# Rotary embedding on one core: a longer fp32 lead of x, and three positions' results stored early in fp32

## The chip, the cores and the metric

One core of one Trainium2 chip. The metric is the device time of one execution in microseconds (us), as a median over executions; for kernels compared here they ran on the same chip in alternating rounds. "Span" is the profiled execution's own length, some 1.7 us shorter than the device time.

## The reference

```python
# x: (8, 2048, 16, 64) float32; cos, sin: (2048, 32)
x1, x2 = x_pairs[..., 0], x_pairs[..., 1]        # even and odd elements
out1 = x1 * cos - x2 * sin
out2 = x1 * sin + x2 * cos
out  = stack([out1, out2], axis=-1)              # same shape as x, float32
```

67.1 MB come in and 67.1 MB go out; each element sees three arithmetic operations.

## The kernel before

A batch of x is a tile of 128 partitions, each with 16 positions of 1024 elements (64 KB of fp32 in memory). Loads and stores go through GpSimd's DMA queue, which casts: fp32 in memory, bf16 on chip. VectorE rotates with three operations for each half of a batch, into a result buffer. There are three buffers for x and three for results. Load b and store b are those of batch b; load 3 reuses the buffer of batch 0, so it is issued only when VectorE is done with batch 0. Exceptions are at the ends: the first positions of batch 0 (the "lead") and the tables come in fp32 over the SP and ACT queues into one of the x buffers, and the last four positions leave in fp32.

A "row" is what one partition gets or gives in one transfer. In the packet records one data packet is one row, and a transfer's 128 rows are 8 for each of the 16 DMA engines. The records call GpSimd's queue q0 ("the software queue"), SP's q1 and ACT's q10. An engine with rows of several queues takes them in turn; a "turn" of q0 is the time of one of its rows.

```python
    with tc.manual_schedule():
        pre = fp32_tile()                            # takes the first x buffer
        ...
        for k in range(HEAD):                        # HEAD = 2: two positions, 4 KB rows
            q = (nc.sync, nc.scalar)[k % 2]
            q.dma_start(out=pre[:, k : k + 1], in_=x_t[0, :, k : k + 1])
        nc.sync.dma_start(out=cos_sb, in_=cos_t)     # tables behind the lead, in `pre` too
        nc.scalar.dma_start(out=sin_sb, in_=sin_t)
        load(0, HEAD)                                # GpSimd queue: rest of batch 0
        load(1)
        nc.scalar.copy(out=xs[0][:, :HEAD], in_=pre[:, :HEAD])
        ...                                          # VectorE builds the bf16 tables
        load(2)                                      # reuses the buffer of `pre`
        for b in range(B):
            os[b] = opool.tile([P, K, HD], bf16, name="ot")
            for k0 in range(0, K, KP):               # KP = 8
                rotate(b, k0, k0 + KP)
            if b + NX < B:
                load(b + NX)                         # reuses the buffer of batch b
            store(b, K if b < B - 1 else K - TAIL)
        ...                                          # the tail: fp32 over SP
```

## Time and profile before

| | before |
|---|---|
| device time | 317.46 us, three runs 317.38 to 317.55 |
| VectorE busy | 212.8 us of a span of 315.7 |
| DMA engines | 16, with work from 1.75 to 314.42 us |
| memory traffic | 134.7 MB, 427 GB/s over the span |

One more view: the DMA issues of the kernel before (destination <- source, issuing queue, count, KB each on the on-chip side, us from issue to landing).

```profile
xt<-in_x_dram ACTq DMA_DIRECT2D x1, 512.0 KB, 5.0
xt<-in_x_dram SPq DMA_DIRECT2D x1, 512.0 KB, 4.9
xt<-in_sin_dram ACTq DMA_DIRECT2D x1, 256.0 KB, 22.7
xt<-in_cos_dram SPq DMA_DIRECT2D x1, 256.0 KB, 18.3
```

The lead lands in 5 us. The tables, half its size and issued 0.4 us later, need 18 and 23: they share the engines with the long rows of GpSimd's queue.

### The profile page before, as it was taken

Reading aid. Unit: us, or ns where it says so; the run is one execution under the profiler, and the core shown is the slowest. Engines: PE = TensorE matmul, PEld = TensorE weight load, DVE = VectorE, ACT = ScalarE, POOL = GpSimd, SP = SyncE. Lnnn points to the kernel's source line nnn. Section 1 sums busy time; section 2 is a strip of 40 time slices with the busy share of each in tenths; the row PEclk is TensorE's granted clock in tenths of the full one; section 3 lists DMA queues with packets and bytes.
Section 4 is the critical chain, followed back from the end, with each engine's and each line's share of the span. In section 5 each row is a group of like instructions: output and inputs, shape, how many; then the busy total and the mean of one; then the engine's idle time right before and its main releaser. Section 6 shows DMA issues by size and latency. Waiting matters only on the chain.

```text
span 315.7 us, 146 instructions
## 1 busy us (share of the span) xinstructions
DVE 212.8 (67%) x51; ACT 6.9 (2%) x4; POOL 8.8 (3%) x20
## 2 busy tenths in 40 slices
DVE  0009999999999999619992299913999049990000
ACT  2100000000000000000000000000000000000400
POOL 1000001000100100100001000000000000000000
DMA  9999999999999999999999999999999999999996
GB/s 269 212 246 203 199 212 253 199 199 237 361 465 332 199 257 407 399 332 262 203 399 440 357 199 199 482 448 266 199 316 415 399 399 523 407 399 457 423 434 280
DMA packets 3024, 101.71 MB, mean 322 GB/s; under 512 B 336, under 2 KB 336, under 8 KB 848
## 3 DMA queue, kind: packets, MB, share of 16 engines
q0 software_dynamic: 2304, 98.04, 97.0%
q1 hardware_dynamic: 432, 2.88, 2.4%
q10 hardware_dynamic: 288, 0.79, 0.6%
HBM read 67.63 MB, written 67.11 MB: 427 GB/s over the span
## 4 chain that ended last, share of the span: by engine, by line
another core or an unknown queue 61%; DMA 16%; DVE 9%; ACT 1%; issue 0%; POOL 0%; ACTq 0%
DMA out_dram<-ot 16%; DVE xt L76 3%; DVE ot L81 3%; DVE ot L75 3%; ACT xt L117 1%; DVE c_tab L100 0%; POOL xt L57 0%; ACTq L116 0%; ACT ot L116 0%; ACTq L117 0%
## 5 line engine op out<-in xcount | busy, mean ns | idle before, releaser
L75 DVE TENSOR_TENSOR ot<-xt,c_tab 128x8192 bf16<-128x8192 bf16 x16 | 70.7, 4420 | 45.8 <-DMA out_dram<-ot 45.7
L81 DVE TENSOR_TENSOR ot<-ot,xt 128x8192 bf16<-128x8192 bf16 x16 | 70.8, 4425 | 0.5
L76 DVE TENSOR_TENSOR xt<-xt,s_tab 128x8192 bf16<-128x8192 bf16 x16 | 70.8, 4425 | 0.5
L98 DVE CAST s_tab<-xt 128x512 bf16<-128x512 f32 x1 | 0.5, 454 | 23.8 <-DMA xt<-in_sin_dram 23.8
L57 POOL DMA_DIRECT2D xt<-in_x_dram x8 | 4.4, 547 | 161.4 <-DVE ot L81 137.4
L60 POOL DMA_DIRECT2D out_dram<-ot x8 | 4.3, 535 | 113.8 <-DVE ot L81 113.8
L116 ACT COPY ot<-ot 1x1 bf16<-1x1 bf16 x1 | 0.2, 193 | 286.6 <-DMA out_dram<-ot 286.6
L117 ACT CAST xt<-ot 128x4096 f32<-128x4096 bf16 x1 | 3.6, 3604 | 0.0
L96 ACT CAST xt<-xt 128x2048 bf16<-128x2048 f32 x1 | 1.9, 1897 | 0.0
L96 ACT ACT_TABLE_LOAD x1 | 1.3, 1283 | 5.7 <-DMA xt<-in_x_dram 5.7
L100 DVE CAST c_tab<-xt 128x1024 bf16<-128x1024 f32 x1 | 0.7, 683 | 0.0
L99 DVE TENSOR_SCALAR s_tab<-xt 128x512 bf16<-128x512 f32 x1 | 0.4, 442 | 0.0
L133 POOL MEMSET const-float32-0.0<- 128x1 f32 x1 | 0.1, 98 | 0.2 <-issue 0.2
L133 POOL MEMSET const-bfloat16-1.0<- 128x1 bf16 x1 | 0.1, 101 | 0.0
L133 POOL MEMSET const-float32-1.0<- 128x1 f32 x1 | 0.1, 98 | 0.0
L133 POOL MEMSET const-uint8-127<- 128x1 uint8 x1 | 0.1, 98 | 0.0
## 6 DMA issues: line engine op xcount, KB each, us to landing
xt<-in_x_dram POOLq DMA_DIRECT2D x7, 4096.0 KB, 42.8
out_dram<-ot POOLq DMA_DIRECT2D x1, 6144.0 KB, 28.0
xt<-in_x_dram POOLq DMA_DIRECT2D x1, 3584.0 KB, 22.8
out_dram<-xt SPq DMA_DIRECT2D x1, 2048.0 KB, 15.5
xt<-in_x_dram ACTq DMA_DIRECT2D x1, 512.0 KB, 5.0
xt<-in_x_dram SPq DMA_DIRECT2D x1, 512.0 KB, 4.9
xt<-in_sin_dram ACTq DMA_DIRECT2D x1, 256.0 KB, 22.7
xt<-in_cos_dram SPq DMA_DIRECT2D x1, 256.0 KB, 18.3
```

Source lines behind the costliest of these rows:

```text
L57: nc.gpsimd.dma_start(out=xs[b][:, k0:], in_=x_t[b, :, k0:])
L60: nc.gpsimd.dma_start(out=out_t[b, :, :k1], in_=os[b][:, :k1])
L75: nc.vector.tensor_tensor(out=rows(op), in0=rows(xp), in1=tab(c_tab), op=mult)
L76: nc.vector.tensor_tensor(out=rows(xp), in0=rows(xp), in1=tab(s_tab), op=mult)
L81: nc.vector.tensor_tensor(out=o3, in0=o3, in1=x_swap, op=add)
L96: nc.scalar.copy(out=xs[0][:, :HEAD], in_=pre[:, :HEAD])
L98: nc.vector.tensor_copy(out=s2[:, :, 0], in_=sin_sb)
L99: nc.vector.tensor_scalar_mul(s2[:, :, 1], sin_sb, -1.0)
L100: nc.vector.tensor_copy(out=c_tab.rearrange("p k (i j) -> p (k i) j", j=2), in_=cos_sb.to_broadcast([P, K * D2, 2]),)
L116: nc.scalar.copy(out=os[B - 2][:1, 0, :1], in_=os[B - 1][:1, K - 1, :1])
L117: nc.scalar.copy(out=tail[:, :TAIL], in_=os[B - 1][:, K - TAIL :])
L133: nc = _bacc.Bacc("TRN2", target_bir_lowering=False, num_devices=1)
```

## The change

What it seems meant to do (the diff doesn't say): use the quick SP and ACT queues for more of the first x, so that VectorE has something to do early, and let the first results leave early, before the casting store of batch 0. The early results are an fp32 copy that ScalarE makes in one of the result buffers. The lead's two transfers now bring two positions each, in rows of 8 KB.

```diff
-    HEAD = 2
+    HEAD = 4
+    LEAD = 3
...
-        for k in range(HEAD):
-            q = (nc.sync, nc.scalar)[k % 2]
-            q.dma_start(out=pre[:, k : k + 1], in_=x_t[0, :, k : k + 1])
+        lead = fp32_tile(opool, "ot")[:, :LEAD]
+        for q, k0 in ((nc.sync, 0), (nc.scalar, HEAD // 2)):
+            q.dma_start(out=pre[:, k0 : k0 + HEAD // 2], in_=x_t[0, :, k0 : k0 + HEAD // 2])
...
-            for k0 in range(0, K, KP):
-                rotate(b, k0, k0 + KP)
+            cuts = [0, KP, K]
+            if b == 0:
+                rotate(b, 0, HEAD)
+                nc.scalar.copy(out=lead, in_=os[b][:, :LEAD])
+                for k in range(LEAD):
+                    nc.sync.dma_start(out=out_t[b, :, k : k + 1], in_=lead[:, k : k + 1])
+                cuts = [HEAD, KP, K]
+            for k0, k1 in zip(cuts, cuts[1:]):
+                rotate(b, k0, k1)
             if b + NX < B:
                 load(b + NX)
-            store(b, K if b < B - 1 else K - TAIL)
+            store(b, LEAD if b == 0 else 0, K if b < B - 1 else K - TAIL)
```

More of the change, by code (lines that the diff above doesn't have):

```diff
@@ L49, with fp32_tile @@
     xs, os = {}, {}
-    def fp32_tile():
-        return xpool.tile([P, K // 2, HD], fp32, name="xt")
+    def fp32_tile(pool, name):
+        return pool.tile([P, K // 2, HD], fp32, name=name)
     def load(b, k0=0):
@@ L57, in load, with store @@
         nc.gpsimd.dma_start(out=xs[b][:, k0:], in_=x_t[b, :, k0:])
-    def store(b, k1=K):
-        nc.gpsimd.dma_start(out=out_t[b, :, :k1], in_=os[b][:, :k1])
+    def store(b, k0=0, k1=K):
+        nc.gpsimd.dma_start(out=out_t[b, :, k0:k1], in_=os[b][:, k0:k1])
     def rotate(b, k0, k1):
@@ L83 @@
     with tc.manual_schedule():
-        pre = fp32_tile()
+        pre = fp32_tile(xpool, "xt")
+        lead = fp32_tile(opool, "ot")[:, :LEAD]
         cos_sb = pre[:, HEAD, : K * D2]
         sin_sb = pre[:, HEAD + 1, : K * D2]
-        for k in range(HEAD):
-            q = (nc.sync, nc.scalar)[k % 2]
-            q.dma_start(out=pre[:, k : k + 1], in_=x_t[0, :, k : k + 1])
+        for q, k0 in ((nc.sync, 0), (nc.scalar, HEAD // 2)):
+            q.dma_start(out=pre[:, k0 : k0 + HEAD // 2], in_=x_t[0, :, k0 : k0 + HEAD // 2])
         nc.sync.dma_start(out=cos_sb, in_=cos_t)
@@ L106 @@
             os[b] = opool.tile([P, K, HD], bf16, name="ot")
-            for k0 in range(0, K, KP):
-                rotate(b, k0, k0 + KP)
+            cuts = [0, KP, K]
[7 more added lines that the diff above has]
+                rotate(b, k0, k1)
             if b + NX < B:
                 load(b + NX)
-            store(b, K if b < B - 1 else K - TAIL)
-        tail = fp32_tile()
+            store(b, LEAD if b == 0 else 0, K if b < B - 1 else K - TAIL)
+        tail = fp32_tile(xpool, "xt")
         nc.scalar.copy(out=os[B - 2][:1, 0, :1], in_=os[B - 1][:1, K - 1, :1])
```

## The prediction

> **What bounds the kernel now.** I read the page first: engine shares, the row of DMA busy tenths, the queues.
>
> ```profile
> DVE 212.8 (67%) x51; ACT 6.9 (2%) x4; POOL 8.8 (3%) x20
> ...
> DMA  9999999999999999999999999999999999999996
> ...
> q0 software_dynamic: 2304, 98.04, 97.0%
> q1 hardware_dynamic: 432, 2.88, 2.4%
> q10 hardware_dynamic: 288, 0.79, 0.6%
> HBM read 67.63 MB, written 67.11 MB: 427 GB/s over the span
> ```
>
> VectorE (DVE) is busy for 67%; the DMA engines are at nine tenths or more in 39 of 40 slices. The row of GB/s swings between about 200 and 523, but that is an artefact: the MB column counts a casting load at its bf16 size. On the HBM side everything moves at 427 GB/s for the whole span. The packet records say the same for one engine: a load row of 64 KB (written as 32 KB of bf16) takes 2.432 us, a store row of 64 KB 2.449, a load row of 56 KB 2.129, a store row of 48 KB 1.83 to 1.85, a 16 KB fp32 row 0.611, a 4 KB fp32 row 0.159, a 2 KB row 0.084. So time goes with the fp32 bytes, about 0.037 ns a byte and 8 ns a packet, whether cast or not and whether software or hardware made the descriptors. I counted the packets in flight: none before 1.75 us, 15.4 of 16 on average from 2 to 4 us, then 16 or more at every stretch up to 312 us (the records of neighbours overlap by some 20 ns, hence 16.16 on average). The last data packet ends at 314.42 us, the span at 315.7. The DMA engines idle some 1.9 us at the start, under 0.15 us from 2 us to 312 us, and the last rows run out unevenly after that.
>
> Second, the waits (who waited for whom: us in total, times, longest), and then three lines of the timeline (start, duration, in brackets the idle time before it): VectorE's start, the load issued at the end of the first batch, the first wait for a result buffer.
>
> ```profile
> POOL xt L57 <- DVE ot L81: 137.4, 5, 35.1
> ...
> DVE ot L75 <- DMA out_dram<-ot: 45.7, 4, 12.1
> DVE s_tab L98 <- DMA xt<-in_sin_dram: 23.8, 1, 23.8
> ```
>
> ```profile
> 23.85 0.45 DVE L98 CAST s_tab<-xt 128x512 bf16<-128x512 f32 x1 [23.85 <-DMA xt<-in_sin_dram]
> ...
> 52.20 0.53 POOL L57 DMA_DIRECT2D xt<-in_x_dram  x1 [25.93 <-DVE ot L81]
> ...
> 140.95 4.42 DVE L75 TENSOR_TENSOR ot<-xt,c_tab 128x8192 bf16<-128x8192 bf16 x1 [9.53 <-DMA out_dram<-ot]
> ```
>
> VectorE waits at two places. It starts at 23.85 because the sine table lands late, and from batch 4 on (140.95, 179.53, 218.23, 256.88) it waits for a result buffer still being stored. Neither costs DMA time: meanwhile the software queue has rows to move. A batch is 39.0 us of DMA (8 rows an engine of 2.432 and 8 of 2.449) against 26.5 us of VectorE (6 of 4.42), so the queue lengthens with every batch. The time is the DMA's total work plus its first 2 us and last 1.3.
>
> **What the Trainium skill says.** (1) "DMA: Bandwidth & Descriptors", section "Where 436 GB/s comes from": 16 ports give 435 GB/s. The trace agrees: 65,536 bytes in 2.432 us on 16 engines is 431, and 427 over the span leaves nothing to win. (2) Same page, "Issuing engines are not separate DMA queues": DMAs from the scalar, sync and gpsimd engines run on the same 16 engines and interleave; several issuers save only issue time. So a second queue for the lead adds no bandwidth. The trace agrees as far as one engine's records go: the 4 KB rows of q1 and q10 alternate, 159 ns each, one at a time. (3) Same page, "Queues, rings and completion order": each engine goes round its queues packet by packet. In the trace a packet record is a whole row, so a small row can wait for a long one: the 2 KB table rows, issued at 1.15 us, take until 16.96 (cosine) and 21.34 us (sine), as each turn of q0 lasts 2.13 us. (4) Same page, "SWDGE vs HWDGE vs iDMA": only DMAs from GpSimd cast. So results that leave over SP need an fp32 copy, here by ScalarE.
>
> **The change, part by part**, in us per DMA engine. 128 rows over 16 engines is 8 rows of each transfer.
> - Lead: 16 rows of 4 KB go (16 x 0.159 = 2.54), 16 rows of 8 KB come (between 0.159 and 0.611 by bytes: 0.310 each, 4.95).
> - First casting load: 56 KB rows (8 x 2.129 = 17.03) become 48 KB (2.129 less a quarter of the step 2.432 - 2.129 for each 2 KB; 1.826 each, 14.61).
> - First store: 64 KB rows (8 x 2.449 = 19.59) become 52 KB (1.84 + 0.25 x 0.61 = 1.99 each, 15.94).
> - Early fp32 stores: 3 x 8 rows of 4 KB, 24 x 0.159 = 3.82.
> - Sum: 39.32 - 39.16 = +0.16. Some extra semaphore packets of 10 to 40 ns make it about 0.2. The bytes in HBM are the same.
>
> So the direct effect is nothing, unless DMA idle time goes away or appears. To take away: between 4 and 6 us I count no idle, so the 1 MB lead already fills the engines until the software queue delivers (first q0 packet at 5.31). A lead twice as long bridges a hole that isn't there. The first 1.9 us are issue latency (SP and ACT issue at 0.74, first packet 1.75) and remain. The tail is unchanged.
>
> To appear: VectorE's schedule moves, and if the software queue runs dry, that costs span.
> - *Start.* The lead takes 4.95 us from 2.0, to about 7. If q0 still joins at 5.3, two or three x rows per queue each wait for a turn of 1.83, and then the tables need 8 turns: 5.3 + 8 x 1.83 + 3 x 2.43 + about 3 of small rows = 30. If q0 joins only behind the lead, at 7.3: 7.3 + 8 x 1.83 + about 1.5 = 23.5, as before. (On one engine six cosine rows ran in succession with sine rows already issued, so rows seem to be committed ahead; I lean to the second.) VectorE starts at 24 to 31.
> - *First batch.* Tables 1.4, then 6 half-size operations of about 2.24 (half of 4.42 plus an estimated 0.03) and 3 full: 26.7 rather than 26.5. It ends at 52 to 60; before, 51.9. ScalarE's early copy of 3072 elements costs 2.75 (between 1.90 for 2048 and 3.60 for 4096) beside VectorE.
> - *First danger.* The work given to the queues without the next load, with the early stores, is 4.95 + 1.4 + 14.61 + 2 x 19.4 + 3.8 + 2 = 65.6, so they are dry at about 65 us. The next load is issued at 52.5 to 60 and needs at most 4 us to its first packet (1.25 to 5.31, the only such time the trace shows). Slack: 1 to 9 us.
> - *Second danger.* The early stores' buffer is handed to batch 2. Their 24 rows and 3 semaphore packets take turns with q0's 64 KB rows, so they need about three q0 transfers (two loads of 20.7 with the small rows, the short store of 17): issued at 36 to 42, first row perhaps 8 us later (the tail, issued at 299.29, had its first row at 305.41), landed at 99 to 111. Batch 2 was ready for its buffer at 79: a new VectorE wait of 15 to 30 us. It then ends at 126 to 138 (before: 104.5), and load 5 is issued there. The queue, with load 4 and store 1, is dry at 140.2. Slack: 13 down to -2 us.
> - From batch 5 on VectorE waits for stores at the same times as before, and the delay is absorbed.
>
> **Rivals.** *A, nothing* (the above): 317.46 + 0.2 = 317.7. For it: an engine never idle and equal bytes. *B, a bubble*: late tables, or early stores landing past 111 us, leave the queue empty for 1 to 8 us: 319 to 325. For it: small rows behind long ones, as the tables show; against: both late-case margins had to go together, and if the queue runs dry early the waiting 4 KB rows fill exactly that hole. *C, faster*: the early stores and an early start of VectorE shorten the end. For it: VectorE begins with smaller pieces and stores begin before 52 us. Against: the DMA has no idle time for earlier stores to use; they displace loads. Only the first 1.9 and last 1.3 us are not DMA work, so even a perfect start gives under 1%. *D, cheaper fp32 rows*: refuted by 0.159 for 4 KB and 0.611 for 16 KB against 2.43 for 64 KB.
>
> **Range and chances.** Centre 317.8: 317.7 with a little for a bubble. Low 317.3 (0.2 below before), high 319.3 (a bubble of 1.5). Over 2% faster would be below 311.1: less than the DMA work. Over 2% slower (above 323.8) needs a bubble of 6 us, both bad cases and more: 3%.
>
> **What would show it.** DMA tenths still 9 from the first slice to the last but one; 427 GB/s; q1 grown by 2.1 MB (0.52 of lead, 1.57 of early stores); a VectorE wait of 15 to 30 us for the early stores ahead of batch 2, with the later buffer waits from batch 5 at about 179.7, 218.4 and 257.1. The early stores take some 60 us from issue to landing. Wrong would be a DMA slice below 9 near 62 or 140 us (B), or q0's rows getting shorter (C or D).

## The result, and the profile after

| | before | after |
|---|---|---|
| device time, median (lowest to highest, 6 runs each) | 317.50 (317.38 to 317.69) | 318.40 (318.19 to 318.61) |
| ratio after / before | | 1.0028, 95% interval 1.0015 to 1.0040 |

The change costs 0.9 us: under 2%, but clear of the noise. The page of the changed kernel, the lines that answer to those shown of before:

```profile
DVE 213.1 (67%) x54; ACT 11.3 (4%) x5; POOL 8.8 (3%) x20
...
DMA  8999999799999999999999999999999999999996
...
q0 software_dynamic: 2304, 95.95, 94.8%
q1 hardware_dynamic: 864, 4.98, 4.2%
q10 hardware_dynamic: 288, 1.31, 1.0%
...
HBM read 67.63 MB, written 67.11 MB: 426 GB/s over the span
```

The DMA engines are nearly as full as before and the bytes are the same. Two digits are new below 9: the 8 of the first slice and the 7 of the eighth (55 to 63 us). A packet counts whole in the slice it starts in, so such a digit is no proof of idle time, only a place to look at. The prediction had named a slice below 9 near 62 us as a sign of rival B. Next the waits and five lines of the timeline: VectorE's start, the issue of the early stores, the issue of load 3 at the end of batch 0, the first operation of batch 2, and the first wait for a result buffer.

```profile
DVE ot L76 <- DMA out_dram<-ot: 36.1, 3, 12.1
DVE s_tab L100 <- DMA xt<-in_sin_dram: 34.0, 1, 34.0
...
ACT L98 <- DMA xt<-in_x_dram: 15.3, 1, 15.3
```

```profile
34.01 0.45 DVE L100 CAST s_tab<-xt 128x512 bf16<-128x512 f32 x1 [34.01 <-DMA xt<-in_sin_dram]
...
45.24 1.30 SPq L114 DMA_DIRECT2D out_dram<-ot  x3
...
62.83 0.53 POOL L58 DMA_DIRECT2D xt<-in_x_dram  x1 [26.40 <-DVE ot L82]
...
88.96 4.42 DVE L76 TENSOR_TENSOR ot<-xt,c_tab 128x8192 bf16<-128x8192 bf16 x1
...
180.49 4.42 DVE L76 TENSOR_TENSOR ot<-xt,c_tab 128x8192 bf16<-128x8192 bf16 x1 [11.93 <-DMA out_dram<-ot]
```

Everything at the start is later, not earlier: VectorE begins at 34.0 instead of 23.9 us, and load 3 is issued at 62.8 instead of 52.2. Batch 2 begins at 88.96 with no idle time in brackets, so the wait that the prediction expected there isn't. From 180 us on the picture is that of before, moved by 1.0 us (179.53 to 180.49).

The DMA issues of the changed kernel show who was slow:

```profile
out_dram<-ot SPq DMA_DIRECT2D x3, 512.0 KB, 21.7
xt<-in_x_dram ACTq DMA_DIRECT2D x1, 1024.0 KB, 14.6
xt<-in_x_dram SPq DMA_DIRECT2D x1, 1024.0 KB, 14.5
xt<-in_sin_dram ACTq DMA_DIRECT2D x1, 256.0 KB, 32.8
xt<-in_cos_dram SPq DMA_DIRECT2D x1, 256.0 KB, 32.6
```

Twice the lead needs three times as long, and behind it the sine table lands 10 us later than before, the cosine table 14. Why is seen in the packet records. They don't name the engine, so I chained them: each record to the one that starts where it ends. One engine of the changed kernel (start, duration in ns, queue, bytes written):

```
5.15 309 q10 8K; 5.46 1828 q0 24K; 7.27 322 q1 8K; 7.59 309 q10 8K; 7.89 1828 q0 24K;
9.70 322 q1 8K; 10.02 309 q10 8K; 10.33 1828 q0 24K; 12.13 322 q1 8K; 12.45 309 q10 8K;
12.76 1828 q0 24K; 14.58 1828 q0 24K; 16.40 84 q10 2K; 16.47 96 q1 2K; ...
```

GpSimd's queue (q0) has its first row at 5.4 us, as before. With 4 KB rows the lead was just finished by then; with 8 KB rows six of 16 are left on this engine, and each remaining pair waits for a 48 KB row of q0. Then the tables begin their own turns: at 16.4 us here, at 14.5 on the earliest engine, against 4.7 before.

And the place near 62 us, on one engine (the chains aren't safe enough over 40 us to say that it is the same):

```
57.63 2431 q0 32K; 60.04 172 q1 4K; 60.21 3439 q0 32K; 63.64 159 q1 4K; 63.79 159 q1 4K;
... (ten rows of 159)
65.51 248 q1 4K; 65.76 376 q1 4K; 66.13 364 q1 4K; 66.49 185 q1 4K; 66.67 159 q1 4K;
66.83 2431 q0 32K; 69.24 2432 q0 32K
```

After the last row of load 2, q0 has no row to run; load 3 is late. The early 4 KB stores, which until then got one turn for each q0 row, run one after another and fill the time. So there is no idle time. But the last row of load 2, with which the engine turns from loads to stores, takes 3.44 us instead of 2.43, and three of the early rows take 0.25 to 0.38 instead of 0.16.

For the account I use two sums from the records of one profile, each over 16 engines: *idle*, the time in 55 to 95 us with fewer than 16 packets in flight, and *stretch*, what rows of 55 to 92 us took above the usual duration of their size. Before has idle 0.00 and stretch 0.73, nearly all of it at 78 to 80 us, where the engines first turn from loads to stores. After has idle 0.01 and stretch 1.44: that turn now lies at 60 us (0.68), and the rows at 64 to 67 us add 0.73. The difference, 0.72, with the 0.16 of the prediction's own sum, is 0.88 of the 0.90 us.

### The profile page after: what moved, and what is told of

Its sections match the earlier page's. It is cut to its first block, busy times and chain, and to the rows that moved or that the text cites. A ratio compares the mean times of both kernels' runs of the same rounds, so it can differ in the third digit from the quotient of the medians. Undisturbed runs are those within 1.5% of the kernel's fastest.

```text
span 316.6 us, 156 instructions
## 1 busy us (share of the span) xinstructions
DVE 213.1 (67%) x54; ACT 11.3 (4%) x5; POOL 8.8 (3%) x20
## 4 chain that ended last, share of the span: by engine, by line
another core or an unknown queue 79%; DMA 10%; DVE 3%; ACT 2%; ACTq 0%; issue 0%; DVEq 0%
DMA xt<-in_sin_dram 10%; ACT xt L126 1%; ACT ot L112 1%; DVE ot L82 1%; DVE ot L76 1%; DVE xt L77 1%; DVE c_tab L102 0%; DVE s_tab L100 0%; ACTq L92 0%; DVE s_tab L101 0%; ACTq L125 0%; ACT ot L125 0%; DVEq L76 0%
## 5 line engine op out<-in xcount | busy, mean ns | idle before, releaser
L76 DVE TENSOR_TENSOR ot<-xt,c_tab 128x8192 bf16<-128x8192 bf16 (+1 forms) x17 | 70.9, 4169 | 36.2 <-DMA out_dram<-ot 36.1
L82 DVE TENSOR_TENSOR ot<-ot,xt 128x8192 bf16<-128x8192 bf16 (+1 forms) x17 | 71.0, 4174 | 0.6
L77 DVE TENSOR_TENSOR xt<-xt,s_tab 128x8192 bf16<-128x8192 bf16 (+1 forms) x17 | 71.0, 4174 | 0.6
L98 ACT CAST xt<-xt 128x4096 bf16<-128x4096 f32 x1 | 3.6, 3604 | 0.0
L112 ACT CAST ot<-ot 128x3072 f32<-128x3072 bf16 x1 | 2.8, 2752 | 22.3 <-DVE ot L82 22.3
## 6 DMA issues: line engine op xcount, KB each, us to landing
xt<-in_x_dram SPq DMA_DIRECT2D x1, 1024.0 KB, 14.5
```

Of the source, the lines that this page charges most:

```text
L76: nc.vector.tensor_tensor(out=rows(op), in0=rows(xp), in1=tab(c_tab), op=mult)
L77: nc.vector.tensor_tensor(out=rows(xp), in0=rows(xp), in1=tab(s_tab), op=mult)
L82: nc.vector.tensor_tensor(out=o3, in0=o3, in1=x_swap, op=add)
L112: nc.scalar.copy(out=lead, in_=os[b][:, :LEAD])
```

## The experiments

Theory 1 after this reading: the larger lead delays the tables and so load 3, and the software queue runs dry at about 62 us; that costs time, or would without the early rows. Rival, theory 2: the early stores themselves are dear (their 4 KB rows took 0.193 us on average, not 0.159). Nine kernels, all correct, rounds of 3 or 5 against the kernel before.

| run | device time, median (before) | ratio, 95% interval | load 3 issued | idle | stretch |
|---|---|---|---|---|---|
| lead_only | 320.13 (317.66) | 1.0077, 1.0064 to 1.0089 | 62.12 | 1.68 | 1.77 |
| lead1 | 319.56 (317.63) | 1.0062, 1.0049 to 1.0074 | 62.52 | 0.68 | 1.92 |
| lead2 | 318.30 (317.63) | 1.0026, 1.0012 to 1.0040 | 62.78 | 0.01 | 1.52 |
| (the change) | 318.40 (317.50) | 1.0028, 1.0015 to 1.0040 | 62.83 | 0.01 | 1.44 |
| lead4 | 318.62 (317.66) | 1.0031, 1.0018 to 1.0044 | 62.58 | 0.01 | 1.18 |
| early_only | 317.77 (317.66) | 1.0002, 0.9989 to 1.0014 | 52.66 | 0.00 | 0.83 |
| tables_first | 317.80 (317.66) | 1.0003, 0.9989 to 1.0017 | 52.41 | 0.00 | 1.06 |
| tables_first_lead_only | 317.50 (317.63) | 0.9997, 0.9984 to 1.0009 | 51.91 | 0.00 | 1.10 |
| tables_first_wide | 317.53 (317.63) | 0.9999, 0.9985 to 1.0012 | 52.51 | 0.00 | 0.02 |
| lead6_only | 322.98 (317.47) | 1.0170, 1.0153 to 1.0187 | 66.80 | 6.18 | 1.90 |

### lead_only: the long lead without the early stores

```diff
-    LEAD = 3
+    LEAD = 0
...
-        lead = fp32_tile(opool, "ot")[:, :LEAD]
...
-                rotate(b, 0, HEAD)
-                nc.scalar.copy(out=lead, in_=os[b][:, :LEAD])
-                for k in range(LEAD):
-                    nc.sync.dma_start(out=out_t[b, :, k : k + 1], in_=lead[:, k : k + 1])
-                cuts = [HEAD, KP, K]
+                cuts = [0, KP, K]
```

> The 2 MB lead alone, no early stores. Theory 1 (the change's early end of the software queue): with the large lead the sine table lands at 34 us, batch 0 ends at 62, load 3 is issued at 62.3 and gives its first row at about 66 us (3.8 us later, as in the changed kernel), but load 2's last row ends at about 62; the early stores, which filled that hole in the changed kernel, are gone. So a real hole of 3.5 to 4 us in the DMA records near 62 to 66 us, and 321.0 to 321.7 us. Theory 2 (the 0.9 us of the change are the price of the early stores themselves, whose 4 KB rows took 0.193 us on average instead of 0.159): without them 317.4 to 317.7 us.

320.13 us: the early stores do not cost the 0.9 us, they save 1.6 of a loss of 2.5. Theory 2 is out. The hole is in the timeline (VectorE's start, issue of load 3) and in the queue line of the window 60 to 70 us (packets, MB, share of 16 engines), here of lead_only:

```profile
33.77 0.45 DVE L99 CAST s_tab<-xt 128x512 bf16<-128x512 f32 x1 [33.77 <-DMA xt<-in_sin_dram]
...
62.12 0.53 POOL L58 DMA_DIRECT2D xt<-in_x_dram  x1 [25.93 <-DVE ot L82]
```

```profile
q0 software_dynamic: 64, 1.57, 79.3%
```

and of the kernel before, same window:

```profile
q0 software_dynamic: 80, 2.10, 97.5%
```

Sixteen packets fewer: each engine misses a row. (The page's row of tenths doesn't show it, for the reason given above.) The size I expected was off by a factor of two (a hole of 1.68 us and 320.13, not 3.5 to 4 and 321.0 to 321.7): load 3's first row came at 63.36, 1.24 us after the issue at 62.12, not 3.8. So in the changed kernel the 3.8 us can't all be latency. As I read the records, load 3 was ready and stood behind 4 KB rows already committed; no run tests that by itself.

### early_only: the early stores with the old lead

```diff
-    HEAD = 4
+    HEAD = 2
+    CUT = 4
-                rotate(b, 0, HEAD)
+                rotate(b, 0, CUT)
-                cuts = [HEAD, KP, K]
+                cuts = [CUT, KP, K]
```

> The early stores alone, lead as before (two 4 KB rows), first rotation of four positions. Both theories: sine table at 23.8 us, batch 0 ends at 52.3, load 3 is in the queue well before load 2 is done, so no hole. Theory 1: 317.5 to 317.7 us, no stretched 4 KB rows; the early stores take turns with the 64 KB rows of the software queue and land only at about 100 us, and VectorE waits some 20 us for their buffer ahead of batch 2 (the wait that my prediction expected of the change and that did not come there). Theory 2: the early rows are costly by themselves, 318.2 to 318.5 us.

317.77 us, no difference to before. Here the wait that the prediction had expected of the change does appear, in the timeline of early_only at batch 2:

```profile
102.60 4.42 DVE L77 TENSOR_TENSOR ot<-xt,c_tab 128x8192 bf16<-128x8192 bf16 x1 [23.73 <-DMA out_dram<-ot]
```

VectorE idles 23.7 us for the buffer of the early stores, whose last landing was at 102.48, and the kernel is no slower: at that time the software queue has work until about 140 us.

### tables_first: the change, with the tables ahead of the lead

```diff
-        for q, k0 in ((nc.sync, 0), (nc.scalar, HEAD // 2)):
-            q.dma_start(out=pre[:, k0 : k0 + HEAD // 2], in_=x_t[0, :, k0 : k0 + HEAD // 2])
         nc.sync.dma_start(out=cos_sb, in_=cos_t)
         nc.scalar.dma_start(out=sin_sb, in_=sin_t)
+        for q, k0 in ((nc.sync, 0), (nc.scalar, HEAD // 2)):
+            q.dma_start(out=pre[:, k0 : k0 + HEAD // 2], in_=x_t[0, :, k0 : k0 + HEAD // 2])
```

> The changed kernel with the two table transfers issued ahead of the x lead on each queue. Theory 1: tables land at about 5 us, the x lead at about 17, ScalarE's cast (1.3 + 3.6) then sets VectorE's start at about 22; batch 0 ends at 49, load 3 is issued at 49.4, no hole: 317.5 to 317.8 us, early stores landing at about 97 us with a wait of VectorE of about 20 us ahead of batch 2. Theory 2: early stores cost the same 0.8 us: 318.2 to 318.5.

317.80 us, with no stretched rows at 60 to 70 us. Its timeline (first rotation, load 3, batch 2):

```profile
25.07 2.29 DVE L76 TENSOR_TENSOR ot<-xt,c_tab 128x4096 bf16<-128x4096 bf16 x1 [19.49 <-ACT xt L98]
...
52.41 0.53 POOL L58 DMA_DIRECT2D xt<-in_x_dram  x1 [26.56 <-DVE ot L82]
...
102.53 4.42 DVE L76 TENSOR_TENSOR ot<-xt,c_tab 128x8192 bf16<-128x8192 bf16 x1 [23.91 <-DMA out_dram<-ot]
```

VectorE and load 3 are 3 us later than expected, but early enough: the order of four transfers takes away the loss, down to 0.1 us, which the noise doesn't tell from nothing. VectorE waits 23.9 us ahead of batch 2, as in early_only, and again no cost of it shows.

### lead4: one more position leaves early

```diff
-    LEAD = 3
+    LEAD = 4
```

> The changed kernel with four positions leaving early instead of three: 8 rows of 4 KB more per engine (1.27 us) to fill the time until load 3's first row, and as much less in store 0. Theory 1: the stretched rows at 65.5 to 66.7 us are the hole in disguise (the queue has too little work until load 3 arrives), so more early rows make up for it: 317.6 to 317.9 us. Theory 2 (the rows are slow by themselves): as the change or longer, 318.4 to 318.8 us.

318.62 us. I had taken the stretched rows for idle time in disguise; then more rows would have helped. They didn't: this form of theory 1 falls. The rows are stretched for another reason, at 65.6 to 66.5 us again (0.37 to 0.43 us each). Two new theories for them: R, a software queue that ran dry costs something on its return, in whichever row is in flight; B, a long burst of stores becomes slow after about 2 us. (In lead_only, too, load 3's first row took 2.6 to 3.4 us instead of 2.43, with no burst before it, which speaks for R.)

### tables_first_lead_only: is it really the tables?

lead_only with the exchange of tables_first.

> The 2 MB lead without early stores, which alone took 320.13 us, but with the tables ahead of it. If the hole of that run comes of the late tables (VectorE's start at 33.8 us, so load 3's issue at 62.1, after load 2's last row), it goes: VectorE starts at about 25, load 3 is issued at about 52, no idle DMA near 62 us, and 317.6 to 317.8 us. If the lead is costly in another way (its 8 KB rows, or the smaller first load), about 320 again.

317.50 us. Same 2 MB lead, same 8 KB rows, no early stores, and the 2.5 us of lead_only are gone. Its timeline (the tables' arrival, the lead's cast on ScalarE, load 3):

```profile
4.01 0.45 DVE L99 CAST s_tab<-xt 128x512 bf16<-128x512 f32 x1 [4.01 <-DMA xt<-in_sin_dram]
...
21.38 3.60 ACT L97 CAST xt<-xt 128x4096 bf16<-128x4096 f32 x1 [2.13 <-DMA xt<-in_x_dram]
...
51.91 0.53 POOL L58 DMA_DIRECT2D xt<-in_x_dram  x1 [26.10 <-DVE ot L82]
```

The lead now lands at about 21 us, because it takes the turns that the tables took. But some of the 16 lead rows were gone before q0 started, and no table waits behind them.

### lead2 and lead1: how many early rows does the hole need?

```diff
-    LEAD = 3
+    LEAD = 2        # lead1: 1
```

> The changed kernel with two positions leaving early. Its early rows end at about 65.2 us, before the stretch of 65.5 to 66.7 us in which rows of the changed kernel took 0.37 us instead of 0.16. Theory R (a software queue that ran dry costs 0.5 to 0.7 us on its return, in whichever row is in flight: load 3's first row in lead_only, the early rows in the changed kernel): 318.1 to 318.4 us, and stretched rows again, now load 3's first ones. Theory B (long bursts of stores become slow after about 2 us): 317.6 to 317.9, nothing stretched at 64 to 67 us.

> The changed kernel with one position leaving early: 8 rows per engine, some 5 of them already gone when load 2 ends at about 62.5 to 63. Both theories: the rest ends at about 63.8, load 3's first row comes at about 64.1 (1.24 us after its issue, as in lead_only), so a hole of some 0.3 us. Theory R: 0.3 plus 0.5 to 0.7, 318.4 to 318.7. Theory B: 0.3 alone plus nothing, 317.9 to 318.1.

lead2, 318.30 us: in time as theory R said, but not in place, since mostly early rows and not load 3's first ones are stretched. They are stretched at 64.6 to 65.5 us, about 1 us into the run of stores, so "after about 2 us" of theory B is wrong. lead1, 319.56: both theories missed. Its early rows end near 63.3 and load 3's first row comes at about 63.8, so the hole is 0.68 us, not 0.3; load 3's first row takes 3.0 to 3.5 us instead of 2.43 on 15 of the 16 engines (as R says); and the first turn from loads to stores stretches by 1.09 us, 0.36 more than before. Together with lead_only and the change that is a series: 0, 1, 2, 3, 4 positions early give 2.5, 1.9, 0.7, 0.9, 1.0 us of loss. Two are enough to cover the hole; what remains is the stretch and some extra work, and the last three losses are too close to rank.

### tables_first_wide: the early stores as one transfer

```diff
-                for k in range(LEAD):
-                    nc.sync.dma_start(out=out_t[b, :, k : k + 1], in_=lead[:, k : k + 1])
+                nc.sync.dma_start(out=out_t[b, :, :LEAD], in_=lead)
```

> tables_first with its three early stores made one, of 12 KB rows: the same bytes in 8 rows per engine instead of 24, so 9 turns instead of 27 beside the software queue. If the number of rows sets their landing, they land at about 60 us instead of 98, VectorE's wait of 24 us ahead of batch 2 goes, and the time stays at 317.6 to 317.9 because that wait was off the path. If bytes set it, landing stays near 98.

317.53 us. The DMA issue line of tables_first, and below it that of tables_first_wide:

```profile
out_dram<-ot SPq DMA_DIRECT2D x3, 512.0 KB, 44.3
```

```profile
out_dram<-ot SPq DMA_DIRECT2D x1, 1536.0 KB, 27.0
```

44.3 is the median of three; the last landed about 67 us after its issue (35.7, and VectorE went on at 102.53). The same bytes in a third of the rows land in 27.0 us, at 61.95 us on the clock, and VectorE's wait ahead of batch 2 is gone. Here rows, not bytes, set how long a small transfer takes beside a queue of long rows. The time is unchanged: the wait was off the path.

### lead6_only: an even longer lead

```diff
-    HEAD = 4
+    HEAD = 6        # in lead_only
```

> lead_only with 3 MB of lead (12 KB rows) instead of 2. If a longer lead only delays the tables (its rows take turns with the software queue's once that has started), the sine table lands some 3 us later than in lead_only (33.8), at about 36 to 38 us: 12 to 13 turns, 8 of 1.53 and 4 to 5 of 2.43 us, with 9 x 0.46 of lead rows and 1.4 of tables from 5.4 us. Load 3 is then issued at about 65, load 2 still ends at about 62, so the hole grows from 1.7 us to about 4.5, and the time from 320.1 to 322.5 to 324 us. If the hole of lead_only has another cause than the tables, about 320 again.

322.98 us, as expected of the tables (six runs, four from 322.62 to 323.08 and two at 324.65 and 325.13; the profile is of the 325.13). Its timeline and its page:

```profile
38.45 0.45 DVE L99 CAST s_tab<-xt 128x512 bf16<-128x512 f32 x1 [38.45 <-DMA xt<-in_sin_dram]
...
66.80 0.53 POOL L58 DMA_DIRECT2D xt<-in_x_dram  x1 [25.93 <-DVE ot L82]
```

```profile
HBM read 67.63 MB, written 67.11 MB: 417 GB/s over the span
```

The hole follows the issue: load 3 at 66.80 plus 1.24, less 61.8 for the end of load 2 (on the earliest engine), is 6.2, and the records have 6.18 us idle. The same sum for lead_only gives 62.12 + 1.24 - 61.8 = 1.6, measured 1.68. The hole is larger than the 4.5 us expected, but the profile is of the slowest run; of the four runs near 322.8 there is no profile. Why this kernel's runs spread over 2.5 us, where all others spread over less than 1, I did not find out.

**The account.** Idle and stretch above those of before, against the measured difference: lead_only 2.7 against 2.5; lead1 1.9 against 1.9; lead6_only 7.4 against 7.7 of the profiled run; the change 0.7, with 0.16 of extra work 0.9, against 0.9. For lead2 it is 0.8, with 0.1 of extra work 0.9, against 1.0 of the profiled run (0.7 of the median). For the runs that never went dry the first turn to stores varies from 0.6 to 1.1 us without a trace in the median (in tables_first_wide it lies at 36 to 41 us, 0.6, outside the window), so single profiles are good to about 0.4 us; lead4 is off by that much (0.5 and 0.2 against 1.0), and its trace shows where: its span runs on for 1.7 us after the last DMA packet, that of before for 1.3.

**What stays open.** In all six kernels in which the software queue ran dry (lead_only, lead1, lead2, the change, lead4, lead6_only), rows were stretched by 0.25 to 0.8 us per engine shortly before or at load 3's return; in the four in which it didn't, by about 0.1 or less at that place. So the stretch goes with the return of the queue and not with the length of the burst. Two simpler readings fall by the records: it isn't the issue of load 3 by itself (in the four others no load row from there to 62 us took over 2.52 us), nor a turn from stores back to loads by itself (lead_only and lead6_only have no stores before it). What in the machine does it no run here separates.

## Why the prediction was right, and where it wasn't

The number was right: 318.40 us in a range of 317.3 to 319.3, 0.6 above its centre. That it stayed in the range is in part luck: VectorE's start was outside the span foreseen, and by itself that late start would have given 320.1 (lead_only); the early rows happened to fill most of the hole. The reason it gave first is confirmed: the bytes are equal, the DMA engines have no idle time to give away, and where the schedule moved without emptying the queue (early_only, tables_first, tables_first_lead_only, tables_first_wide) the time stayed within 0.15 us of before. The steps, in its order:

- **Direct effect, +0.16 to 0.2.** Not contradicted, but too small to be shown: early_only and tables_first, with the early stores and no dry queue, were 0.1 longer, with intervals of 0.4 us either way.
- **"A lead twice as long bridges a hole that isn't there."** Holds, and it is worse than useless with the tables behind it.
- **Start: "I lean to the second"** (q0 joins only behind the lead, tables at 23.5). Wrong: q0's first row came at 5.38, as before, in the middle of the lead. The other branch, "= 30", was right in kind and 4 us short. On most engines five q0 rows ran before the first table row, where I had counted three, and twelve before the last sine row, where I had counted eleven; the rest is small rows. The sine landed at 34.0, outside "24 to 31".
- **First batch "ends at 52 to 60".** It ended at 62.5, from that error.
- **First danger, "slack: 1 to 9 us".** Load 3 was issued at 62.8, later than the 52.5 to 60 of the prediction, and q0 ran dry: load 2's last rows ended at 63.2 to 64.1, load 3's first began at 66.6 to 67.8. The engines had work in between only because the early rows, which the 65.6 includes, were left to fill the time. Without them (lead_only) the hole is 1.7 us. The 4 us to a first row were too many: 1.24 once the queue was empty.
- **Second danger, "a new VectorE wait of 15 to 30 us".** Not in the change: batch 2 began at 88.96 with no wait, because the dry queue let all early rows through by 67.8 (last landing 70.5). The mechanism is real: with the queue never dry the wait was 23.7 (early_only) and 23.9 us (tables_first). Two of its sums don't come out as written: 36 to 42, plus 8, plus 20.7 + 20.7 + 17 is 102 to 108, not "99 to 111" (102.5 and 102.4 in those two runs), and 140.2 less 126 less 4 is a slack of 10, not 13.
- **Rival B, "the waiting 4 KB rows fill exactly that hole".** This is what happened, and it is why 320.1 became 318.4.
- **The term not in the sum: 0.7 us of stretched rows** when load 3 came back. It has the size of the difference between the 317.7 worked out and the 318.4 measured, as far as one profile can say (0.4 us).

So the two parts of the change pull against each other: the long lead costs 2.5 us, the early stores give back 1.6 of it, by accident of where they lie. Alone, the early stores are neutral within the noise; with the tables sent first, so is the lead. No version beat the kernel before clearly: the best, tables_first_lead_only and tables_first_wide, stand at 0.9997 and 0.9999 with intervals across 1.

## What to carry to other kernels

When the DMA engines are full from end to end, ask of a change first two things: does it change the bytes, and can any queue run dry. Waits of VectorE of 24 us cost nothing here, because the queue had work beyond them. Small transfers that everything waits for (tables, masks) go first on their queue, ahead of bulk, since in these runs, once a queue of long rows had started, further rows waited for its turns, and a transfer's landing went by its number of rows. And work out how long the queue lasts against the issue of the next load: here a table 10 us late moved that issue past the end, and the loss was nearly the difference of two times read from the profile.

## What the Trainium skill lacked or had wrong

- "DMA: Bandwidth & Descriptors", "Latency and other measured facts", gives about 1 us to the first byte for DMAs from GpSimd. lead_only agrees when the queue is empty in mid-kernel (1.24 us), but at the start of the kernel it was 4.1 us (issue at 1.25, first row at 5.38), whether a 1 MB or a 2 MB lead ran beside it; the page doesn't have that case.
- The same page, "Queues, rings and completion order", has engines switch at packets of typically 9 to 17 descriptors. In these records a turn is a whole row, up to 64 KB and 2.43 us (how many descriptors that is, they don't show); no page warns that an early issue on another queue doesn't help a transfer of many short rows (24 rows of 4 KB: last landing at 102.48 after issue at 35.9; 8 rows of 12 KB: 27.0 us).
- No page has the cost of the first turn from loads to stores (0.5 to 1.3 us of stretched rows per engine over all eleven profiles), nor that of a software queue's return after running dry (0.25 to 0.8 us).
